# Encoder layer on one core: the filters' second product over 128 rows, and three side products one unit of weights later

## The chip, the cores and the metric

The kernel runs on one core of one Trainium2 chip. The metric is the device time of one execution in microseconds (us). Before the change it is 1980.1 us, the median of three runs (1979.52, 1980.10 and 1980.14 us). The engines are named as the profile names them: PE is the matrix engine's multiplication, PEld its loading of weights, DVE the vector engine, ACT the scalar engine, POOL the GpSimd engine, and SP the engine whose queue issues most transfers.

## What is computed

One layer of an encoder over 256 tokens of 2048 channels, in float32. Cut to its steps:

```
x <- LN1(alpha*x + 0.5*(silu(x@Wg1) * (x@Wu1)) @ Wd1)         # d_ff 5632
h = x;  proj = h @ w_in                                       # 2048 x 6144
v, g1, g2 = split(short_conv(proj[:, :3072]), 3)              # the Hyena group, 1024 channels each
filt = sin-MLP(33 -> 64 -> 64 -> 64)(positions) @ filt_w_out  # 64 x 4096, times a decay
y = v;  for n in 0, 1:  y = g[n] * fftconv(y, filt[n, forward], filt[n, backward], bias[n])
o = differential attention of the other half of proj          # 8 heads
x <- LN2(alpha*x + [rms(y) ; o] @ w_out)
x <- LN3(alpha*x + 0.5*(silu(x@Wg2) * (x@Wu2)) @ Wd2)
```

## The kernel before

All matrices are streamed once from DRAM in 656 **units** of 0.5 MB, in the order of their use. SP's queue fetches a unit (`fetch`, five ahead), and `prepare` splits it three units ahead of its use into a high part (a cast on ACT, L159) and a low part (raw minus high, on DVE, L160). There are four buffers each for the high and the low part, so ACT cannot cast a unit before the unit four places ahead of it has been used up. PE then makes three products of every float32 product: high x high, low x high and high x low.

Work that is not part of the stream is written as Python generators. `tick`, called once for each unit, counts down what a generator last yielded and runs its next piece when the count is 0. So `yield 2` means: let two units pass. A piece's products stand on PE's queue between two units, and PE takes its queue strictly in order. Within that, a scheduler that works by its own estimates sets the exact order on each engine.

Two places matter here.

**The filters** (`filter_gen`) run beside the down projection of the first feed-forward half step. `h` holds the network's 64 outputs for 256 positions twice, in partitions 0 to 63 and again in 64 to 127; `hs` holds its high part in the lower-numbered half and its low part in the other. `fh` and `fl` are the high and low parts of `filt_w_out`, which is loaded into both halves too. For each of eight blocks (four blocks of channels `cc`, two orders `n`) there are two directions `d` and two token halves `j`, and for each of these four a product over all 128 rows (L550), which gives high x high + low x high at once, and then a product over the first 64 rows alone (L551), which gives high x low. All eight of a block stand together on PE's queue. After them DVE multiplies by the decay (L553), and `spectra_mm` takes the filters to the frequency domain (tiles `pr`, `pi`, named `prk`, `pik` here), in twelve products over 128 rows by 256 columns.

**The Hyena group** takes 48 units (`hy<cc>_<s>_<kq>`: four blocks of channels `cc`, in each the sections `s` = 0 for v, 1 for the first gate and 2 for the second, of four units each). `conv_in` (L636 on) makes the short convolution of a section on ACT and DVE (tile `z`, L648), yields, and transposes it on PE into `pt` (L657). For s = 0 it then starts `chain(cc)`: `product("a")` with the first filter, an inverse transform on PE into `py`, a gate, `product("b")` with the second filter, and an inverse transform into `pz` (L725, L726). `product` is: the transform on PE (`pra`, `pia` or `prb`, `pib`), a butterfly on ACT and DVE (`ab`, `cd`), the multiplication by the filter's spectrum, half on POOL (`t2`, `t3`) and half on DVE (`t0`, `t1`), and the real and imaginary results, split into `rh`, `rl`, `ih`, `il` (ACT casts at L97, DVE subtractions at L94). After the last split it yields 3 before the inverse transform. A chain is longer than the 12 units of a block of channels, so product b of one block and product a of the next run side by side, and since `rh`, `rl`, `ih`, `il` have one buffer each, the a product cannot be split before `pz` of the block ahead has been computed.

Of the kernel before, what the change touches and what calls it, by code (L numbers as in the profile page):

```python
# [11 lines left out]
F32 = mybir.dt.float32  # L12
# [16 lines left out]
HID = 64  # L29
EPS = 1e-5  # L30
ALPHA = 2.0 ** 0.25
# [13 lines left out]
def _constants():  # L45
    """Tables that depend on shapes alone. Tokens are cut as l = 2 p + j."""
    f4 = np.float32
    lag = 2 * np.arange(P)[:, None] + np.arange(2)[None, :]
    t = np.linspace(0.0, 1.0, L, dtype=f4)[:, None]
    bands = (EMB - 1) // 2  # L50
    w = f4(2.0 * math.pi) * np.arange(L, dtype=f4)[:, None] / f4(L)
    fr = np.linspace(1e-4, bands - 1, bands, dtype=f4)[None, :]
    z = np.concatenate([t, np.cos(fr * w), -np.sin(fr * w)], axis=-1)
    z_t = np.ascontiguousarray(z[lag.T.reshape(-1)].T, dtype=f4)
    lo, hi = math.log(1e-2) / 1.5, math.log(1e-2) / 0.3
    deltas = np.abs(np.linspace(lo, hi, DH, dtype=f4))
    decay = np.exp(-t * deltas)[lag].astype(f4)
    om = 2.0 * math.pi * (np.arange(P) + 0.5) / NFFT
    ang = lag.T[:, :, None].astype(np.float64) * om[None, None, :]
    fwd = np.stack([np.cos(ang), -np.sin(ang)], axis=1)  # L60
    fwd = np.ascontiguousarray(fwd.transpose(2, 0, 1, 3).reshape(P, 4 * P), dtype=f4)
    inv = np.stack([np.cos(ang), -np.sin(ang)], axis=0) * (2.0 / NFFT)
    inv = np.ascontiguousarray(inv.transpose(3, 0, 1, 2).reshape(P, 4 * P), dtype=f4)
    fi = f4(ROPE_THETA) ** (-np.arange(0, ROT, 2, dtype=f4) / f4(ROT))
    an = (lag.astype(f4)[:, :, None] * fi[None, None, :]).astype(f4)
    cs, sn = np.cos(an), np.sin(an)
    rope = np.stack([np.concatenate([cs, cs], -1), np.concatenate([-sn, sn], -1)], axis=1)
    rope = np.repeat(rope[:, :, :, None, :], 8, axis=3)
    rope = np.ascontiguousarray(rope.reshape(P, 2 * 2 * 8 * ROT), dtype=f4)
    return {"c_zt": z_t, "c_decay": np.ascontiguousarray(decay), "c_fwd": fwd, "c_inv": inv, "c_rope": rope}  # L70
# [3 lines left out]
def kernel(ctx: ExitStack, tc: tile.TileContext, a: dict, out: bass.AP):  # L74
    nc = tc.nc
# [24 lines left out]
    def after(ins, first):  # L100
        """Keeps ins behind first in their engine's queue."""
        tc.add_manual_dep(ins.ins, first.ins.name, mybir.DependencyInfo(mybir.DependencyClass.NoSync, mybir.DependencyReason.DATA), reason="order")
# [3 lines left out]

# [1 line left out]
    units = []  # L108

    def ws_units(tag, w, c0, ws=None):  # L110
        """[4 k-tiles x 256 columns] of one matrix, or of several in turn."""
        for kq in range(KD // 4):
            for m, v in enumerate(ws or [w]):
                units.append((v[0][kq * 512:(kq + 1) * 512, c0:c0 + 256].rearrange("(k p) c -> p k c", p=P), 4, 256, f"{tag}_{kq}_{m}"))

    def as_units(tag, w, c0, kt):
        """[2 k-tiles x 512 columns]."""
        for ku in range(kt // 2):
            units.append((w[0][ku * 256:(ku + 1) * 256, c0:c0 + 512].rearrange("(k p) c -> p k c", p=P), 2, 512, f"{tag}_{ku}"))
# [46 lines left out]

    # work that goes on beside the stream: generators that yield how many units to let pass
    side = []
# [32 lines left out]

# [1 line left out]
    res = const.tile([P, 2, D], F32, name="res")  # L203
# [12 lines left out]

    # per-channel vectors, as columns
    NCONV = 24
# [59 lines left out]
    def warm(n):  # L278
        """Keeps the array's clock up over a wait; the products are not used."""
        ps = bank("ps_warm")  # L280
        for _ in range(n):
            mm(out=ps[:, :P], lhsT=ones, rhs=ones, start=True, stop=True)

    def scale_residual(tag, g, b):
        """res = ALPHA * (res * g + b), or ALPHA * res."""
        for c in range(4):
# [36 lines left out]
    def last_rows(tag, pd, scale):  # L323
        """The last columns of a row block, and its statistics; the first token tile goes ahead."""
        ln = []
        for j in range(2):
            add_rows(pd[j], j, 3, scale)
            ln.append(ln_stats(tag, j))
        if tag == "2":
            warm(WARM)  # L330
        return ln
# [14 lines left out]
    def ws_block(ps, h, lo, kq, between=None):  # L346
        """Left half: hi x hi + lo x hi; right half: hi x lo."""
        for k in range(4):
            kk = kq * 4 + k
            if k == 2 and between is not None:  # L350
                between()
            for t in range(2):
                ts_ = slice(t * P, (t + 1) * P)
                mm(out=ps[t], lhsT=h[:, k, ts_], rhs=xx[:, kk].rearrange("p a l -> p (a l)"), start=kk == 0, stop=False)  # L354
                mm(out=ps[t][:, :L], lhsT=lo[:, k, ts_], rhs=xx[:, kk, 0, :], start=False, stop=kk == KD - 1)  # L355
# [5 lines left out]
    def as_block(pd, lhs, use, n_k):  # L361
        """Rows on the partitions: [tokens, 512 columns]; lhs(k, j) gives the split tokens."""
        for j in range(2):
# [6 lines left out]
    def as_chunk(pd, lhs, n_k, lead=1):  # L370
        """The first token tile is done with the last `lead` units before the second one is."""
        n = n_k // 2
# [4 lines left out]

# [1 line left out]
    def ffn(tag, first, down_side=None, gate_side=None, filler=None, lead=2):  # L379
# [41 lines left out]

# [1 line left out]
    spec = dr.tile([NCC, P, 2, 2, 2 * CH], F32, name="spec")  # L423
# [6 lines left out]
    def spectra_mm(fw_hi, fw_lo, parts_, tag):  # L430
        """[ReE | ReO] and [ImE | ImO] of the transform at half-odd frequencies."""
        pr, pi = bank(f"pr{tag}"), bank(f"pi{tag}")
# [6 lines left out]
    def butterfly(pr, pi, ro, ab, cd):  # L439
        """ab = [Re+ | Re-], cd = [Im+ | Im-]."""  # L440
        nc.scalar.copy(out=ro[:, 0, :], in_=pr[:, CH:])
# [53 lines left out]
    def filter_gen():  # L495
        """Per block of channels and order: the two filters, the even and odd parts about lag 0, their spectra."""
        fw_hi = blk(14).rearrange("p k l -> p (k l)")
# [21 lines left out]
        nc.vector.tensor_copy(out=hs[:HID], in_=hs_hi[:HID].bitcast(F32))  # L519
        sub(nc.vector, hs[HID:], h[HID:], hs_hi[HID:])  # L520
        yield 3
        ft()
# [14 lines left out]
        for i, (cc, n) in enumerate(todo):  # L537
# [7 lines left out]
            for d in range(2):  # L545
                ps = bank(f"pf{i}_{d}")
                for j in range(2):
                    js = slice(j * P, (j + 1) * P)
                    po = ps[:, j * CH:(j + 1) * CH]
                    mm(out=po, lhsT=hs[:, js], rhs=fh[:, d, :], start=True, stop=False)  # L550
                    mm(out=po, lhsT=hs[:HID, js], rhs=fl[:HID, d, :], start=False, stop=True)  # L551
                t = t512(f"fa{i}_{d}")
                nc.vector.tensor_tensor(out=t.rearrange("p j c -> p (j c)"), in0=ps, in1=dec.rearrange("p j c -> p (j c)"), op=ALU.mult)  # L553
                ab.append(t)
            # lag 0 of the backward filter is not used (its sine is 0 too): the skip bias takes its place
            nc.gpsimd.dma_start(out=ab[1][0:1, 0, :], in_=a["hyena_bias"][:, n, cs])
# [20 lines left out]

# [1 line left out]
    def first0(c):  # L579
# [22 lines left out]

# [1 line left out]
    mix = ctx.enter_context(ExitStack())  # L604
# [27 lines left out]
    def conv_in(cc, s, ps):  # L632
        """Short convolution of one block of channels; v and the first gate go to [token, channel]."""
        z = hp.tile([P, 2, 2, P], F32, tag="z2" if s == 2 else "z", name=f"z{cc}_{s}", bufs=2)
# [15 lines left out]
        if s == 2:  # L650
            z2s[cc] = z
            return
        yield 2 if cc == s == 0 else 1
        pt = bank(f"pt{cc}_{s}")
# [13 lines left out]
    def product(tag, u, n):  # L668
        """Spectrum of u times the filter's, as what the even and the odd tokens take of it, split."""
        pr, pi = spectra_mm(fw_hi, fw_lo, (u, u), tag)  # L670
# [24 lines left out]
        split(*i, v[1])  # L695
        yield 3
        prod[tag] = (r, i)
# [3 lines left out]
    def chain(cc, u):  # L701
# [16 lines left out]
        load_spec(cc + 1, 1)  # L718
        # [high | low] parts of the table side by side
        pz = [bank(f"pz{cc}_{t}").rearrange("p (j a l) -> p j a l", j=2, a=2) for t in range(2)]  # L720
# [22 lines left out]
    def rms_rows(sqs, n, tag):  # L743
        """1 / rms per token of the sum of squares over the partitions, in all partitions (PSUM)."""
        ps = bank(f"pss{tag}")
# [60 lines left out]

    # differential attention
    yah = mixp.tile([P, 8, L], F32R, name="yah")
# [130 lines left out]

    # output projection  # L940
    def wo_lhs(k, j):
# [24 lines left out]
    mix.close()  # L966
# [1 line left out]
    ln2 = ln  # L968
# [66 lines left out]
```

## Time and profile before

| | |
|---|---|
| median of three runs | 1980.1 us |
| span of the profiled execution | 1978.4 us |
| PE busy | 1944.3 us (98%) |
| DVE busy | 1217.0 us (62%) |
| ACT busy | 925.6 us (47%) |
| POOL busy | 307.0 us (16%) |
| granted clock, mean | 0.996 of full speed |

The span is from the first to the last instruction; 1.7 us of the median lie around it. Times of rows are counted from the span's start. A row of a timeline gives start, duration, engine, line, operation, tiles and sizes, and in brackets how long the engine was idle before it and what ended that. Products on PE overlap: what one costs in a row of others is the distance from its start to the next start, not the duration that the row gives.

### The profile page before, as it was taken

To read this page: it belongs to the slowest core of one execution; us is meant where nothing else is said; L and a number is where in the kernel's file an instruction comes from. 1 tells how busy PE (TensorE), PEld (TensorE's weight loads), DVE (VectorE), ACT (ScalarE), POOL (GpSimd) and SP (SyncE) were. 2 spreads that over 40 slices of the span, in tenths; PEclk is the share of its full clock that TensorE was granted. 3 is DMA by queue.
4 is the path that set the end of the run, shared out by engine and by line. 5 is a ranking of instruction groups with operands and counts; after the bars stand their busy time and mean duration, and the time that the engine had idled before them with its cause. 6 is when DMAs were issued, how large, how long until landed. Compare 5 with 4: busy or idle time off the path is not lost. (4 is left out here: it accounts for less than half of the span.)

```text
span 1978.4 us, 27114 instructions
## 1 busy us (share of the span) xinstructions
PE 1944.3 (98%) x10292; PEld 1661.0 (84%) x10292; DVE 1217.0 (62%) x1534; ACT 925.6 (47%) x1332; POOL 307.0 (16%) x330
## 2 busy tenths in 40 slices
PE   9999999999999999999999999999999999999996
PEld 7888888888887777888878888888888888888885
DVE  5555556555565655899978666755555555544445
ACT  5444444544444434555555544545444544433332
POOL 5112111121100000212321010311111121100001
PEclk9999999999999999999999999999999999999998
DMA  7666666666666655755575544866666666656663
GB/s 244 189 189 191 192 191 195 190 187 192 194 201 196 202 177 177 237 186 170 173 235 151 160 155 149 279 191 192 188 192 189 190 190 192 190 183 191 189 186 104
DMA packets 293514, 374.33 MB, mean 189 GB/s; under 512 B 13103, under 2 KB 222152, under 8 KB 293384
## 3 DMA queue, kind: packets, MB, share of 16 engines
q1 hardware_dynamic: 288648, 359.80, 59.1%
q0 software_dynamic: 4736, 12.82, 2.1%
q8 instruction: 80, 1.31, 0.3%
q14 instruction: 50, 0.41, 0.1%
HBM read 364.18 MB, written 8.39 MB: 188 GB/s over the span
## 5 line engine op out<-in xcount | busy, mean ns | idle before, releaser
L354 PE MATMUL ps<-xx,hi1g 128*128 128x512 f32 x1408 | 489.5, 391 | 1.3 <-DVE xx L94 0.8
L354 PE MATMUL ps<-xx,hi2g 128*128 128x512 f32 x1408 | 488.6, 391 | 1.1 <-DVE xx L94 1.1
L355 PE MATMUL ps<-xx,lo1g 128*128 128x256 f32 x1408 | 397.4, 282 | 0.3 <-DVE lo1g L160 0.3
L355 PE MATMUL ps<-xx,lo2g 128*128 128x256 f32 x1408 | 397.3, 282 | 0.0
L160 DVE TENSOR_TENSOR lo2g<-raw2g,hi2g 128x1024 fp32r<-128x1024 f32 x176 | 235.1, 1337 | 179.4 <-ACT hi2g L159 179.4
L160 DVE TENSOR_TENSOR lo1g<-raw1g,hi1g 128x1024 fp32r<-128x1024 f32 x176 | 231.5, 1317 | 180.0 <-ACT hi1g L159 179.8
L354 PEld LDWEIGHTS ps<-xx,hi1g 128*128 128x128 f32 x1408 | 264.3, 188 | 57.6 <-DVE xx L94 1.4
L354 PEld LDWEIGHTS ps<-xx,hi2g 128*128 128x128 f32 x1408 | 264.2, 188 | 55.8 <-ACT xt L268 1.3
L159 ACT CAST hi2g<-raw2g 128x1024 fp32r<-128x1024 f32 x176 | 185.2, 1053 | 186.6 <-PE ps L354 176.1
L159 ACT CAST hi1g<-raw1g 128x1024 fp32r<-128x1024 f32 x176 | 185.3, 1053 | 184.8 <-PE ps L354 175.6
L355 PEld LDWEIGHTS ps<-xx,lo1g 128*128 128x128 f32 x1408 | 266.7, 189 | 0.6 <-DVE lo1g L160 0.6
L355 PEld LDWEIGHTS ps<-xx,lo2g 128*128 128x128 f32 x1408 | 266.8, 189 | 0.1
L160 DVE TENSOR_TENSOR lo2d<-raw2d,hi2d 128x1024 fp32r<-128x1024 f32 x88 | 108.5, 1233 | 128.2 <-ACT hi2d L159 128.2
L390 POOL TENSOR_TENSOR hf<-hf,sg 128x256 f32<-128x256 f32 x88 | 65.6, 766 | 765.7 <-DVE hf L359 765.6
L159 ACT CAST hi1d<-raw1d 128x1024 fp32r<-128x1024 f32 x88 | 92.4, 1050 | 155.0 <-PE pd L91 145.1
L159 ACT CAST hi2d<-raw2d 128x1024 fp32r<-128x1024 f32 x88 | 92.6, 1052 | 148.8 <-PE pd L91 145.4
L160 DVE TENSOR_TENSOR lo1d<-raw1d,hi1d 128x1024 fp32r<-128x1024 f32 x88 | 107.7, 1223 | 83.4 <-ACT hi1d L159 83.4
L89 PE MATMUL pd<-hi1d,hh 128*128 128x512 f32 x352 | 140.3, 399 | 0.0
L90 PE MATMUL pd<-lo2d,hh 128*128 128x512 f32 x352 | 139.4, 396 | 0.0
L91 PE MATMUL pd<-hi2d,hl 128*128 128x512 f32 x352 | 139.4, 396 | 0.0
L89 PE MATMUL pd<-hi2d,hh 128*128 128x512 f32 x352 | 139.3, 396 | 0.0
L91 PE MATMUL pd<-hi1d,hl 128*128 128x512 f32 x352 | 139.3, 396 | 0.0
(371 smaller groups left out, 3073.2 us busy)
## 6 DMA issues: line engine op xcount, KB each, us to landing
raw1g<-in_ffn_w_gate_dram SPq DMA_DIRECT2D x88, 512.0 KB, 3.5
raw1g<-in_ffn_w_up_dram SPq DMA_DIRECT2D x88, 512.0 KB, 3.6
raw1d<-in_ffn_w_down_dram SPq DMA_DIRECT2D x88, 512.0 KB, 3.7
raw2g<-in_ffn_w_gate_dram SPq DMA_DIRECT2D x88, 512.0 KB, 3.5
raw2g<-in_ffn_w_up_dram SPq DMA_DIRECT2D x88, 512.0 KB, 3.5
raw2d<-in_ffn_w_down_dram SPq DMA_DIRECT2D x88, 512.0 KB, 3.9
rawhy<-in_w_in_dram SPq DMA_DIRECT2D x48, 512.0 KB, 3.6
rawat<-in_w_in_dram SPq DMA_DIRECT2D x48, 512.0 KB, 3.9
```

The costliest lines, as they stand in the source:

```text
L89: mm(out=o, lhsT=lh, rhs=rh, start=start, stop=False)
L90: mm(out=o, lhsT=lh, rhs=rl, start=False, stop=False)
L91: mm(out=o, lhsT=ll, rhs=rh, start=False, stop=stop)
L159: i1 = nc.scalar.copy(out=hi, in_=raw)
L160: i2 = nc.vector.tensor_tensor(out=lo, in0=raw, in1=hi.bitcast(F32), op=ALU.subtract)
L354: mm(out=ps[t], lhsT=h[:, k, ts_], rhs=xx[:, kk].rearrange("p a l -> p (a l)"), start=kk == 0, stop=False)
L355: mm(out=ps[t][:, :L], lhsT=lo[:, k, ts_], rhs=xx[:, kk, 0, :], start=False, stop=kk == KD - 1)
L390: nc.gpsimd.tensor_tensor(out=hf, in0=hf, in1=sg, op=ALU.mult)
```

## The change

The diff also empties comments and docstrings, and four lines added behind L520 give later lines numbers that are higher by four. What is left:

```diff
@@ filter_gen
         nc.vector.tensor_copy(out=hs[:HID], in_=hs_hi[:HID].bitcast(F32))
         sub(nc.vector, hs[HID:], h[HID:], hs_hi[HID:])
+
+        hz = xx[:, 1, 0, :]
+        nc.vector.memset(hz[HID:].bitcast(F32), 0.0)
+        nc.vector.tensor_copy(out=hz[:HID], in_=hs_hi[:HID].bitcast(F32))
         yield 3
...
                     mm(out=po, lhsT=hs[:, js], rhs=fh[:, d, :], start=True, stop=False)
-                    mm(out=po, lhsT=hs[:HID, js], rhs=fl[:HID, d, :], start=False, stop=True)
+                    mm(out=po, lhsT=hz[:, js], rhs=fl[:, d, :], start=False, stop=True)
@@ conv_in
-        yield 2 if cc == s == 0 else 1
+        yield 3 if cc == s == 0 else 2
         pt = bank(f"pt{cc}_{s}")
@@ product
         split(*i, v[1])
-        yield 3
+        yield 4
         prod[tag] = (r, i)
```

The second product now runs over all 128 rows, of which the lower 64 hold zeros in `hz`. The transposes `pt` stand one unit later on PE's queue, and the inverse transforms `py` and `pz` one unit later after their product. What follows them moves along: `chain` starts one unit later, and its end three units later.

Three places on the queues show it. The first is on PE, at the first transposes of the Hyena group. Before:

```order
L354 MATMUL ph0_1_1_6923<-xx_70,hihy0_1_3_0_6961 128x512
L355 MATMUL ph0_1_1_6923<-xx_70,lohy0_1_3_0_6962 128x256
L657 MATMUL pt0_0_7045<-ident_83,z0_0_6934 128x128 x4
L354 MATMUL ph0_2_0_7035<-xx_70,hihy0_2_0_0_6991 128x512
L355 MATMUL ph0_2_0_7035<-xx_70,lohy0_2_0_0_6992 128x256
```

and with the change:

```order
L354 MATMUL ph0_2_1_7038<-xx_70,hihy0_2_0_0_6993 128x512
L355 MATMUL ph0_2_1_7038<-xx_70,lohy0_2_0_0_6994 128x256
L661 MATMUL pt0_0_7078<-ident_83,z0_0_6936 128x128 x4
L354 MATMUL ph0_2_0_7037<-xx_70,hihy0_2_1_0_7015 128x512
L355 MATMUL ph0_2_0_7037<-xx_70,lohy0_2_1_0_7016 128x256
```

The transposes stood behind unit `hy0_1_3` and stand behind the next one, `hy0_2_0`.

The second is on DVE, where product b of the first block of channels (`abb0`, `cdb0`) meets product a of the second (`aba1`, `cda1`). Before:

```order
L443 TENSOR_TENSOR abb0_7556<-prb0_7519,rob0_7555 128x256
L444 TENSOR_TENSOR abb0_7556<-prb0_7519,rob0_7555 128x256
L445 TENSOR_TENSOR cdb0_7557<-rob0_7555,pib0_7520 128x256
L446 TENSOR_TENSOR cdb0_7557<-rob0_7555,pib0_7520 128x256
L681 TENSOR_TENSOR t0b0_7607<-abb0_7556,res_69 128x512
L682 TENSOR_TENSOR t1b0_7608<-cdb0_7557,res_69 128x512
L691 TENSOR_TENSOR t2b0_7609<-t2b0_7609,t3b0_7610 128x512
L160 TENSOR_TENSOR lohy2_0_2_0_7604<-rawhy2_0_2_0_7483,hihy2_0_2_0_7603 128x1024
L443 TENSOR_TENSOR aba1_7618<-pra1_7569,roa1_7617 128x256
L444 TENSOR_TENSOR aba1_7618<-pra1_7569,roa1_7617 128x256
```

and with the change:

```order
L443 TENSOR_TENSOR abb0_7632<-prb0_7567,rob0_7631 128x256
L444 TENSOR_TENSOR abb0_7632<-prb0_7567,rob0_7631 128x256
L445 TENSOR_TENSOR cdb0_7633<-rob0_7631,pib0_7568 128x256
L446 TENSOR_TENSOR cdb0_7633<-rob0_7631,pib0_7568 128x256
L359 TENSOR_TENSOR pc19_7651<-ph1_2_1_7424,pc19_7651 128x256
L685 TENSOR_TENSOR t0b0_7681<-abb0_7632,res_69 128x512
L686 TENSOR_TENSOR t1b0_7682<-cdb0_7633,res_69 128x512
L443 TENSOR_TENSOR aba1_7643<-pra1_7586,roa1_7642 128x256
L444 TENSOR_TENSOR aba1_7643<-pra1_7586,roa1_7642 128x256
```

A unit of weights was prepared between the two (`lohy2_0_2`, L160); now they follow each other directly. On PE's queue `prb0` stood behind unit `hy1_2_1` and `pra1` behind `hy1_2_2`; now both stand behind `hy1_2_3`. For the pairs b1 with a2 and b2 with a3 the distance was two units and is now one.

The third is on PE, where `pz` of the first block of channels ends and `py` of the second follows. Before, the end of `pz0`:

```order
L725 MATMUL pz0_1_7806<-iv_6739,ihb0_7707 128x256
L726 MATMUL pz0_1_7806<-iv_6739,ilb0_7708 128x256
L354 MATMUL ph2_1_0_7765<-xx_70,hihy2_1_1_0_7738 128x512
L355 MATMUL ph2_1_0_7765<-xx_70,lohy2_1_1_0_7739 128x256
L354 MATMUL ph2_1_1_7766<-xx_70,hihy2_1_1_0_7738 128x512
L355 MATMUL ph2_1_1_7766<-xx_70,lohy2_1_1_0_7739 128x256
```

and with the change:

```order
L729 MATMUL pz0_1_7884<-iv_6741,ihb0_7764 128x256
L730 MATMUL pz0_1_7884<-iv_6741,ilb0_7765 128x256
L89 MATMUL py1_7902<-rha1_7733,iv_6741 128x256
L661 MATMUL pt2_0_7915<-ident_83,z2_0_7775 128x128 x4
L354 MATMUL ph2_2_0_7874<-xx_70,hihy2_2_0_0_7832 128x512
L355 MATMUL ph2_2_0_7874<-xx_70,lohy2_2_0_0_7833 128x256
L354 MATMUL ph2_2_1_7875<-xx_70,hihy2_2_0_0_7832 128x512
L355 MATMUL ph2_2_1_7875<-xx_70,lohy2_2_0_0_7833 128x256
L354 MATMUL ph2_2_0_7874<-xx_70,hihy2_2_0_0_7832 128x512
L355 MATMUL ph2_2_0_7874<-xx_70,lohy2_2_0_0_7833 128x256
L90 MATMUL py1_7902<-rla1_7734,iv_6741 128x256
```

Before, all sixteen products of unit `hy2_1_1` stood between the end of `pz0` and the first product of `py1`; now the first product of `py1` follows `pz0` at once, and the second one comes after four transposes and six products of a unit.

## Rows read from the trace of the kernel before

**Rows 1.** Busy time of the engines by stretch: down projection, Hyena group
```profile
core 0: us, PE busy (x) PEld busy (x) DVE busy (x) ACT busy (x) POOL busy (x), PEclk, DMA share, GB/s
497.00:700.00 203.00, 203.00 (x897) 161.35 (x896) 122.11 (x152) 84.77 (x106) 14.52 (x24) 1.00 0.64 196
812.00:960.00 148.00, 142.42 (x862) 126.81 (x861) 142.37 (x262) 80.02 (x129) 29.41 (x21) 1.00 0.58 179
```

**Rows 2.** Waits of PE: line waited for, us in total, times, longest
```profile
PE pt L657 <- DVE z L648: 4.5, 2, 2.6
...
PE py L90 <- DVE rla L94: 1.1, 1, 1.1
...
PE pw L900 <- DVE e L896: 1.0, 1, 1.0
```

**Rows 3.** Timeline of PE at the first of eight filter blocks
```profile
515.68 0.40 PE L91 MATMUL pd<-hi1d,hl 128*128 128x512 f32 x1
515.91 0.28 PE L550 MATMUL pf<-xx 128*128 128x256 f32 x1
516.12 0.38 PE L551 MATMUL pf<-xx 64*128 64x256 f32 x1
516.43 0.38 PE L550 MATMUL pf<-xx 128*128 128x256 f32 x1
...
518.00 0.38 PE L551 MATMUL pf<-xx 64*128 64x256 f32 x1
518.31 0.50 PE L89 MATMUL pd<-hi1d,hh 128*128 128x512 f32 x1
518.65 0.39 PE L90 MATMUL pd<-lo1d,hh 128*128 128x512 f32 x1
```

**Rows 4.** Tile `pf`: duration in ns (least, median, most), first and last start
```profile
L551 PE MATMUL pf<-xx x32: 380/382/383, 516.1 to 695.2; 64*128 64x256 f32 x32
```

**Rows 5.** Timeline of PE at the twelve products of a spectrum
```profile
532.41 0.28 PE L89 MATMUL prk<-xx 128*128 128x256 f32 x1
...
533.72 0.28 PE L91 MATMUL pik<-xx 128*128 128x256 f32 x1
533.84 0.40 PE L89 MATMUL pd<-hi1d,hh 128*128 128x512 f32 x1
```

**Rows 6.** Timeline of PE's weight loads, in the same spectrum
```profile
532.53 0.19 PEld L91 LDWEIGHTS prk<-xx 128*128 128x128 f32 x1
532.64 0.19 PEld L89 LDWEIGHTS prk<-xx 128*128 128x128 f32 x1
```

**Rows 7.** Timeline of PE at attention scores, products over 64 rows
```profile
1024.20 0.28 PE L90 MATMUL psc<-ql,qh 64*128 64x256 f32 x1
1024.32 0.28 PE L91 MATMUL psc<-qh,ql 64*128 64x256 f32 x1
1024.53 0.50 PE L89 MATMUL pa0v<-hiat,xx 128*128 128x512 f32 x1
```

**Rows 8.** Timeline of DVE where `hs` is made
```profile
488.23 0.28 DVE L519 CAST xx<-xx 64x256 fp32r<-64x256 f32 x1
```

**Rows 9.** Timeline of ACT ahead of the first convolution
```profile
810.50 0.62 ACT L97 CAST fw_hi<-c_fwd_raw 128x512 fp32r<-128x512 f32 x1 [4.81 <-DMA c_fwd_raw<-in_c_fwd_dram]
```

**Rows 10.** Timeline of DVE, then of PE: a low part made, and first used
```profile
876.23 1.22 DVE L160 TENSOR_TENSOR lohy<-rawhy,hihy 128x1024 fp32r<-128x1024 f32 x1
...
878.95 0.28 PE L355 MATMUL ph<-xx,lohy 128*128 128x256 f32 x1
```

**Rows 11.** Timeline of ACT at `py1`
```profile
885.72 0.62 ACT L97 CAST rha<-v0a 128x512 fp32r<-128x512 f32 x1
```

**Rows 12.** Timeline of DVE in the first burst
```profile
863.71 1.78 DVE L682 TENSOR_TENSOR t1b<-cdb,res 128x512 f32<-128x512 f32 x1
865.42 0.68 DVE L691 TENSOR_TENSOR t2b<-t2b,t3b 128x512 f32<-128x512 f32 x1
```

**Rows 13.** Timeline of POOL in the first burst
```profile
863.19 1.75 POOL L680 TENSOR_TENSOR t3b<-cdb,res 128x512 f32<-128x512 f32 x1
```

## Prediction, made before the changed kernel was run

> **What bounds the kernel now.** I first read busy time by stretch [rows 1]. In the down projection, where the filters are made, PE is busy for all of its 203.00 us, at the full granted clock (1.00, the 2.4 GHz level): there any time taken from PE's queue comes off the end, as long as DVE (122.11 us) and the transfers (a share of 0.64) keep up, and both have room. In the Hyena group PE is busy for 142.42 of 148 us, so it loses 5.6 us there, and DVE is busy for 142.37 us: the second engine is nearly full. Then I read PE's waits [rows 2]: two of the transposes `pt` wait for the convolution (4.5 us together, the longest 2.6), `py` once for the low part of its operand (1.1 us), the weights of attention `pw` once (1.0 us). Behind the first layer norm these are the only waits of 1 us and more up to the output projection, and the change touches the first two. Last I read single rows of PE where the filters stand [rows 3], since a busy PE need not be a PE at its pace.
>
> **The second product over 128 rows.** A block's eight products run from 515.91 to 518.31 us: 2.40 us, 0.30 each. The products ahead of them come every 0.23 us (515.68 to 515.91) though they have twice the columns. The product behind them costs 518.65 - 518.31 = 0.34 us instead of 0.23 [rows 3]. What makes them slow? The twelve products of a spectrum have the same 256 columns, all over 128 rows: 532.41 to 533.84 us, 1.43 us, 0.119 each [rows 5]. Nor are 64 rows slow by themselves: the attention scores have 64 rows too, and two in a row are 0.12 us apart (1024.20 to 1024.32), but the last one, ahead of a product over 128 rows, takes 0.21 (1024.32 to 1024.53) [rows 7]. So the price lies in changing from 128 rows to 64 and back, about 0.1 us or more each time, and a block changes eight times. With 128 rows throughout I price the eight as the spectrum's: 8 x 0.119 = 0.95 us, and the product behind them at 0.23. Saved: (2.40 - 0.95) + (0.34 - 0.23) = 1.56 us a block. The 32 products over 64 rows are alike to 3 ns (380 to 383) [rows 4], four to a block, so eight blocks save 8 x 1.56 = **12.5 us**, all on the path. The bounds are 0 (rival 3 below) and these 12.5, which leave no change of shape in a block; I take 12.5, since the spectrum's row is of the same shape in the same stage.
>
> The change adds a memset and a cast of 64 x 256 to DVE, once. The nearest row is the cast of that size, 0.28 us [rows 8]; two make 0.6 us, ahead of the next unit's low part. DVE is idle for 80 us of the 203 us that follow, and low parts are made three units ahead, so I cost it at nothing; without that cover it would be 0.6 us. The memset waits until the gate products have read block 1 of `xx`, as the instructions ahead of it already wait for block 0, so nothing new is queued behind it.
>
> Here a rule of the Trainium skill speaks against the change; the rows of the same stage come first. In the spectrum a load of weights takes 0.19 us and the next one starts 0.11 us after it began, while products run without a break [rows 5, 6]: loads over 128 rows do lie beside products over 128 rows. The Trainium skill, page "TensorE: Matmul & The Clock Gate", section "Part 3: Packing small matmuls — row/col tiling", says that a load of weights overlaps a product in flight only when the two use different row groups. By that rule the trace of the spectrum could not look as it does.
>
> **The side products one unit later.** A unit is sixteen products in pairs of 0.23 + 0.12 us, 2.8 us. The two waits of `pt` (2.6 and 1.9) are each shorter than that, and DVE's order ahead of these convolutions is the same. The first comes from ACT, which stood for 4.81 us waiting for a table's transfer [rows 9] with the convolution queued behind it; that transfer is issued at the same unit as before. So both waits go: **-4.5 us**, with 0.2 left over at most.
>
> Against it stands what moves together. Product b0 used to start one unit ahead of product a1; now both start behind the same unit (second place of the change). Their work on DVE comes as one burst, in the stretch where DVE is full. Before, that burst cut the lead of the low parts to 878.95 - (876.23 + 1.22) = 1.5 us [rows 10]. Now b0 comes two units later against the stream and a1 one, and the units' due times stay. If the burst ends one unit (2.8 us) later, the lead becomes 1.5 - 2.8 = -1.3: PE waits **1.3 us** for a low part (bounds 0 and 3). Then `py1` follows `pz0` with no unit between (third place). Its operand `rha1` has one buffer, read by `pz0` to its end, so ACT casts it only then: 0.62 us [rows 11] and the way there and back, **0.8 us**. The next product of `py1` needs `rla1`, behind which DVE may be on time (0) or three low parts late (3 x 1.13 = 3.4, each row of 1.22 overlapping the next by 0.09); I take the middle, **1.7 us**. Sum 3.8 us, against 1.1 us for the wait shown plus about 0.5 in smaller gaps of the same `py1` now: a net loss of **2.2 us** (from -1.6 to +3.9 or so). The order of DVE's queue was made by the scheduler for this, which is why the second product of `py1` stands behind six of a unit: that hides part of it.
>
> The pairs b1/a2 and b2/a3 come one unit apart, as b0/a1 was, but their `pz` and `py` stand a unit later than that one's did, which is more than the 1.6 us that it lost: 0, with 1.6 each as the upper bound. The chain's end, three units later, falls further into the attention heads; the 1.0 us of `pw` may go or double: 0 (from -1 to +1). Transfers move with their generators (the spectra of the next block of channels and the reload of `res` on SP's queue); the spectra keep over four units until they are read, so they cost nothing. No stretch here is idle long enough to have lost the clock before: it stood at 1.00 over the 148 us with the 2.6 us wait in them [rows 1].
>
> Sum: -12.5 - 4.5 + 2.2 = -14.8. The profiled span is 1978.4 us, 1.7 less than the median of the runs; I take the difference off the median: 1980.1 - 14.8 = **1965.3 us**.
>
> **The rivals.** (1) *The bursts cost nothing.* If DVE keeps up, `py1` loses its 1.6 us as well and `pw` its 1.0: -12.5 - 7.1, 1960.5 us. For it: leads of low parts are far longer outside the bursts. Against it: DVE's 142.37 of 148 us. (2) *The bursts cost more.* All upper bounds: -12.5 - 4.3 + 3.9 + 3.2 + 1.0 = -8.7, 1971.4 us. For it: while POOL multiplies, DVE's multiplications slow down, 1.78 us against 0.68 for the same size once POOL is through [rows 12, 13], and POOL's work for two products now comes in one go. (3) *The filters gain nothing.* If a load over 128 rows has to wait for the product before it, each of the eight costs 0.19 + 0.12 = 0.31 us, a block 2.48, and only the side products' 2.3 us are left: 1977.8 us. That is the time by the rule of the Trainium skill named above; [rows 5, 6] speak against it. (4) *Slower.* DVE becomes the bound of the Hyena group: POOL's two products hold the memory path for 6.1 us in each of the three bursts, and six operations of DVE there take 1.1 us more each (1.78 against 0.68, rows 12), 6.6 us a burst, and every `py` waits as `py1` did, 1.6. That decides once the low parts' lead is used up at a burst's start. 3 x 8.2 = 24.6, less 12.5 and 4.5: +7.6, 1987.7 us. Against it: the lead was never below 1.5 us, and only the first pair falls together entirely.
>
> **How the numbers follow.** A measurement of this kernel can tell about 0.2% (4 us) from no change. The forecast, 1962.5 to 1968.5 us: 58%. Rival 1, below that: 14%. Rival 2, 1968.5 to 1975: 21%. Rival 3: 4%. Rival 4: 3%. The range from 1961 to 1971.5 us leaves out some half of rival 1, a quarter of rival 2, and rivals 3 and 4: 19%. Faster by over 0.2% are the forecast and rivals 1 and 2: 0.93; same is rival 3: 0.04; slower is rival 4: 0.03.
>
> **What would show it.** In the timeline of PE at the filters all eight products should show 128 rows and lie 0.12 us apart, a block 0.95 us, the product behind it 0.23. A block of 2.4 us would prove rival 3 and cost 12.5 us. In the waits, `pt <- z` should be gone; `py` should wait for `rha` and `rla`, once each, some 0.8 and 1.7 us, at `py1` alone; waits of L355 for a low part ahead of `pz0` should be near 1.3 us. If `py` waits in all of the last three blocks, the sum of the bursts was too small; if none is left, rival 1 holds. A granted clock below 1.00 in the Hyena group would mean a wait long enough to cost PE its clock, which I have not priced.

## The result and the profile after

The median is **1966.53 us** (1966.24 to 1968.11, four runs) against 1979.91 us (1979.52 to 1980.14, four runs) of the kernel before on the same chip: the ratio is 0.993, with a 95% interval from 0.9918 to 0.9941. The kernel is faster by 13.4 us; 14.8 were forecast, and the time lies inside the range. The profiled execution has a span of 1964.9 us, 13.5 less than before.

In the kernel after, the two products of a block are L554 and L555, `pt` is L661, `pz` L729 and L730, `pw` L904.

First PE at the first filter block (start, duration, engine, line, operation, tiles, sizes):

```profile
515.74 0.39 PE L91 MATMUL pd<-hi1d,hl 128*128 128x512 f32 x1
515.97 0.28 PE L554 MATMUL pf<-xx 128*128 128x256 f32 x1
516.09 0.28 PE L555 MATMUL pf<-xx 128*128 128x256 f32 x1
...
516.80 0.28 PE L555 MATMUL pf<-xx 128*128 128x256 f32 x1
516.92 0.40 PE L89 MATMUL pd<-hi1d,hh 128*128 128x512 f32 x1
517.16 0.39 PE L90 MATMUL pd<-lo1d,hh 128*128 128x512 f32 x1
```

Against [rows 3], all eight products show 128 rows. They take 516.92 - 515.97 = 0.95 us instead of 2.40, and the product behind them 517.16 - 516.92 = 0.24 us instead of 0.34. So a block saves 1.55 us, and eight of them 12.4.

The loads of weights of the same eight products (engine PEld):

```profile
515.97 0.19 PEld L555 LDWEIGHTS pf<-xx 128*128 128x128 f32 x1
516.09 0.19 PEld L554 LDWEIGHTS pf<-xx 128*128 128x128 f32 x1
516.21 0.19 PEld L555 LDWEIGHTS pf<-xx 128*128 128x128 f32 x1
```

A load of 0.19 us starts every 0.12 us, each together with a product that uses the weights loaded before, over the same 128 rows. The rule on which rival 3 stood (the Trainium skill, page "TensorE: Matmul & The Clock Gate", section "Part 3: Packing small matmuls — row/col tiling": a load overlaps a product in flight only when their row groups differ) does not hold here; by it the block would have cost some 2.5 us.

The loads of the kernel before, at the same place, look different:

```profile
516.12 0.18 PEld L551 LDWEIGHTS pf<-xx 64*128 64x128 f32 x1 [0.25 <-issue]
516.43 0.19 PEld L550 LDWEIGHTS pf<-xx 128*128 128x128 f32 x1
```

There each load starts only with the product that uses it (516.12 and 516.43, as the products of [rows 3]), and not with the product ahead of it. So where the number of rows changes, the load lies open: 0.18 to 0.19 us each time, and with the 0.12 us of the product 0.31. That is the sum that rival 3 made for the kernel after; it was the kernel before that paid it.

Then the waits of PE in the kernel after (line waited for, us in total, times, longest):

```profile
PE py L89 <- ACT rha L97: 1.9, 1, 1.9
...
PE pw L904 <- DVE e L900: 1.6, 1, 1.6
PE py L90 <- DVE rla L94: 1.5, 1, 1.5
...
PE ph L355 <- DVE lohy L160: 0.5, 1, 0.5
```

Against [rows 2], the 4.5 us of `pt` are gone. New are the first line (at `py1`) and the last (a low part ahead of `pz0`). The wait of `py` for `rla` has grown from 1.1 to 1.5 us and stands at another place, `py2`. `pw` went from 1.0 to 1.6.

Last the busy times by stretch (PE, PEld, DVE, ACT, POOL, granted clock, DMA share, GB/s). The Hyena group begins 12 us earlier than before, so the 148 us are taken from 800 on:

```profile
497.00:700.00 203.00, 203.00 (x950) 167.43 (x949) 128.21 (x159) 89.67 (x111) 14.57 (x24) 1.00 0.67 208
800.00:948.00 148.00, 144.02 (x868) 127.94 (x867) 141.81 (x262) 80.85 (x129) 27.07 (x21) 1.00 0.58 177
```

In the down projection PE stays the bound while more work passes in the same 203 us: x950 instructions instead of x897 [rows 1]. In the Hyena group PE is busy for 144.02 us instead of 142.42; DVE is still the second full engine (141.81).

**How the rest of the difference is found.** The idle time that a wait shows is less than what PE loses there. In a row of others a product over 256 columns is followed after 0.119 us by the next start, one over 512 columns after 0.233, and a transpose by the next one after 0.109. What a start lies behind that is called *lost* below. Here are PE's rows at the two places where `py` waits now; first `py1`:

```profile
877.20 0.28 PE L730 MATMUL pz<-iv,ilb 128*128 128x256 f32 x1
879.39 0.39 PE L89 MATMUL py<-rha,iv 128*128 128x256 f32 x1 [1.91 <-ACT rha L97]
879.62 0.60 PE L661 MATMUL pt<-ident,z 128*128 128x128 f32 x4
...
880.98 0.28 PE L355 MATMUL ph<-xx,lohy 128*128 128x256 f32 x1
881.33 0.39 PE L90 MATMUL py<-rla,iv 128*128 128x256 f32 x1
```

Lost: 879.39 - 877.20 - 0.12 = 2.07 us for `rha`, and 881.33 - 880.98 - 0.12 = 0.23 us for `rla`. Ahead of `pz0`, a product of a unit loses 872.75 - 871.86 - 0.233 = 0.66 us to its low part, here on PE and then on DVE:

```profile
871.86 0.39 PE L354 MATMUL ph<-xx,hihy 128*128 128x512 f32 x1
872.75 0.38 PE L355 MATMUL ph<-xx,lohy 128*128 128x256 f32 x1 [0.50 <-DVE lohy L160]
...
871.49 1.21 DVE L160 TENSOR_TENSOR lohy<-rawhy,hihy 128x1024 fp32r<-128x1024 f32 x1
```

The sum at this pair is 2.96 us. Why `rha` came so late is seen on ACT in the same stretch:

```profile
878.18 0.37 ACT L358 COPY pc<-ph 128x256 f32<-128x256 f32 x1 [0.65 <-DVE z L652]
878.45 0.38 ACT L734 COPY zs<-pz 128x256 f32<-128x256 f32 x1
878.71 0.63 ACT L97 CAST rha<-v0a 128x512 fp32r<-128x512 f32 x1
```

The cast of `rha` was not next on ACT's queue when `pz0` had ended: two copies stood ahead of it, and the first of them waited 0.65 us for DVE's convolution. Then `py2`, on PE and on DVE:

```profile
920.25 0.28 PE L89 MATMUL py<-rha,iv 128*128 128x256 f32 x1
922.02 0.39 PE L90 MATMUL py<-rla,iv 128*128 128x256 f32 x1 [1.50 <-DVE rla L94]
```

```profile
919.03 2.34 DVE L160 TENSOR_TENSOR lohy<-rawhy,hihy 128x1024 fp32r<-128x1024 f32 x2
921.30 0.68 DVE L94 TENSOR_TENSOR rla<-v0a,rha 128x512 fp32r<-128x512 f32 x1
```

PE loses 1.65 us, since DVE made two low parts of units, 2.34 us, ahead of `rla`. With 0.14 us at `ila`, a few products further on, the pair costs 1.8 us.

### The profile page after: what moved, and what is told of

Same layout as the page of the kernel before. It is cut to its first block, busy times and chain, and to the rows that moved or that the text cites. A ratio compares the mean times of both kernels' runs of the same rounds, so it can differ in the third digit from the quotient of the medians.

```text
span 1964.9 us, 27112 instructions
## 1 busy us (share of the span) xinstructions
PE 1932.7 (98%) x10292; PEld 1656.2 (84%) x10292; DVE 1215.2 (62%) x1536; ACT 925.8 (47%) x1332; POOL 306.0 (16%) x330
## 5 line engine op out<-in xcount | busy, mean ns | idle before, releaser
L160 DVE TENSOR_TENSOR lo2g<-raw2g,hi2g 128x1024 fp32r<-128x1024 f32 x176 | 235.1, 1337 | 179.3 <-ACT hi2g L159 177.7
L160 DVE TENSOR_TENSOR lo1g<-raw1g,hi1g 128x1024 fp32r<-128x1024 f32 x176 | 232.2, 1320 | 178.8 <-ACT hi1g L159 178.8
L160 DVE TENSOR_TENSOR lo2d<-raw2d,hi2d 128x1024 fp32r<-128x1024 f32 x88 | 108.3, 1231 | 128.3 <-ACT hi2d L159 128.3
L160 DVE TENSOR_TENSOR lo1d<-raw1d,hi1d 128x1024 fp32r<-128x1024 f32 x88 | 107.2, 1222 | 71.0 <-ACT hi1d L159 71.0
```

What stands on the lines that cost most here:

```text
L160: i2 = nc.vector.tensor_tensor(out=lo, in0=raw, in1=hi.bitcast(F32), op=ALU.subtract)
```

## The experiments

Three questions were put: what each half of the change does by itself, what makes the filter products slow, and what makes the side products wait.

### Each half alone

e1 keeps the filters' change and leaves both yields as they were before. Against the kernel before:

```diff
+        hz = xx[:, 1, 0, :]
+        nc.vector.memset(hz[HID:].bitcast(F32), 0.0)
+        nc.vector.tensor_copy(out=hz[:HID], in_=hs_hi[:HID].bitcast(F32))
...
-                    mm(out=po, lhsT=hs[:HID, js], rhs=fl[:HID, d, :], start=False, stop=True)
+                    mm(out=po, lhsT=hz[:, js], rhs=fl[:, d, :], start=False, stop=True)
```

> The kernel before with the second filter product over 128 rows, and the three yields as they were. Theory (the price lies in changing from 128 rows to 64 and back): eight blocks of 1.56 us each go from PE's path and nothing else moves, so 12.4 us less than before, about 1967.5 us; the two waits of pt (4.5 us), the one of py1 (1.1) and that of pw (1.0) stay. Rival (part of those 12.4 us was slack that the faster down projection hands to a later wait): 1969 to 1972 us, with a new wait of PE for a unit of weights behind the filters.

Measured: 1969.28 us (1967.67 to 1970.61, five runs) against 1981.73 of the kernel before (1979.64 to 1984.03, 15 runs of this chip, with which e1 to e4 are compared); ratio 0.9937 (0.9925 to 0.995). The medians are 12.45 us apart, what the filter blocks give. The expected 1967.5 us had been reckoned from the 1979.9 us of the runs beside the result. The span of the profiled execution is 1967.1 us, 11.3 less than before. `pt` waits twice and `py` once, as in the kernel before:

```profile
PE pt L661 <- DVE z L652: 3.7, 2, 1.9
...
PE py L90 <- DVE rla L94: 1.1, 1, 1.1
```

So no new wait behind the filters takes anything back. In this execution part of the 12.4 us is given back elsewhere: the first filter block starts 0.7 us later (516.59 us), and behind the first wait of `pt` PE ran some 3 us at the lower level of its clock (last section).

e2 makes only the other half, both yields, in the kernel before:

```diff
-            yield 2 if cc == s == 0 else 1
+            yield 3 if cc == s == 0 else 2
...
-        yield 3
+        yield 4
```

> The kernel before with the three yields raised and the filter products as they were. Theory (the waits of pt go, 4.7 us by starts of products, but the bursts give 3.5 us back: py1 +1.3, py2 +1.8, pw +0.6, py3 -0.3): 1.0 to 1.3 us less than before, about 1978.8 us. Rival (the yields bring their full 4.5 to 5 us, and the filters bring less than 12.4): about 1975.2 us.

Measured: 1980.43 us (1979.07 to 1981.64, 11 runs); ratio 0.9995 (0.9986 to 1.0004). No change can be told, and the 1.0 to 1.3 us that were expected of the side products' move can't be ruled out either. Its waits repeat those of the kernel after, to the tenth:

```profile
PE py L89 <- ACT rha L97: 1.9, 1, 1.9
...
PE py L90 <- DVE rla L94: 1.5, 1, 1.5
```

In its profiled execution the side products lose 4.74 us from the Hyena group to the end of the last `py`, the kernel before 6.80 and the kernel after 4.93, so 2.1 us are gained there, and 0.6 of them go to `pw`. That the span was 1978.5 us nevertheless comes from 775 to 800 us, where PE's granted clock was 0.93 and in the kernel before 1.00, ahead of anything that the yields move.

### One yield at a time, beside the filters

e3 keeps `hz` and the yields of `conv_in`, and takes the product's back to 3. e4 keeps `hz` and the product's yield of 4, and takes those of `conv_in` back. Against the kernel after:

```diff
 # e3
-        yield 4
+        yield 3
 # e4
-            yield 3 if cc == s == 0 else 2
+            yield 2 if cc == s == 0 else 1
```

> The changed kernel with the yield of product back at 3; the transposes stay one unit later. Theory (what the product's yield does is to push the pairs b0/a1, b1/a2 onto each other or next to py, and it costs): no wait of py2, py1 about 1.6 us as before the change, no wait of pt, so about 2 us less than the changed kernel, 1964.3 us. Rival (the bursts come from the transposes' yield, since it starts the chains later): the waits of py1 and py2 stay at 3 and 1.8 us, time as the changed kernel's 1966.5 or above, since pz and py come a unit earlier.

> The changed kernel with the yields of conv_in back at 2 and 1; the inverse transforms stay one unit later. Theory: the waits of pt are back (2.6 and some of the 1.9 us), and the burst of b0 with a1 stays, so 12.4 us less than before and then 0 to 3 us more: 1968 to 1971 us. Rival (the bursts come from the transposes' yield): py1 and py2 wait for nothing, 1966 us or less.

Measured, e3: **1963.10 us** (1963.02 to 1963.31, four runs), ratio 0.9906 (0.9893 to 0.992); span 1961.2 us, 3.7 less than the kernel after. e4: 1971.75 us (1969.28 to 1972.18, five runs), ratio 0.9947 (0.9935 to 0.996); span 1967.5 us. Against e1, on the same chip, the yields of `conv_in` gain 6.2 us and the product's yield costs 2.5. So the yields of `conv_in` are the whole gain, and the product's yield is a loss. (e4 lies 0.75 us above the range expected; its profiled execution was the fastest of the five, at a mean granted clock of 0.996 where the other four had 0.995.) The waits of e3:

```profile
PE py L90 <- DVE rla L94: 1.0, 2, 0.9
```

and of e4:

```profile
PE pt L661 <- DVE z L652: 2.4, 1, 2.4
...
PE py L90 <- DVE rla L94: 1.8, 3, 0.8
PE py L89 <- ACT rha L97: 1.7, 1, 1.7
```

Without the product's yield `py` no longer waits for `rha` at all, and `pt` does not wait either. With that yield alone, `py` waits in all of the last three blocks and `pt` still once.

### What makes the filter products slow

e5 is the kernel before with the same products over 128 and 64 rows, in another order: two over 128 rows, then two over 64, and this twice. A block then changes its number of rows four times instead of eight. The lines added:

```diff
+            pss = [bank(f"pf{i}_{d}") for d in range(2)]
+            for j in range(2):
+                js = slice(j * P, (j + 1) * P)
+                for d in range(2):
+                    mm(out=pss[d][:, j * CH:(j + 1) * CH], lhsT=hs[:, js], rhs=fh[:, d, :], start=True, stop=False)
+                for d in range(2):
+                    mm(out=pss[d][:, j * CH:(j + 1) * CH], lhsT=hs[:HID, js], rhs=fl[:HID, d, :], start=False, stop=True)
```

> The kernel before with the eight products of a block in another order: per token half two products over 128 rows (one per direction), then two over 64 rows. The shape changes four times a block instead of eight; all products stay as they are, and the yields too. Theory (a change of shape costs): half of the 1.56 us a block goes, 0.75 us, 6 us in all, about 1974 us; two products of equal shape in a row lie 0.12 us apart. Rival (each product over 64 rows is slow by itself, in this stage): all eight stay 0.3 us apart or the 64-row ones do, 1978 to 1980 us.

Measured: 1974.83 us (1972.29 to 1975.84, six runs) against 1979.94 (1978.87 to 1982.77, ten runs); ratio 0.9967 (0.9955 to 0.9979). PE at the first block (x2 is two products in one row):

```profile
516.16 0.40 PE L549 MATMUL pf<-xx 128*128 128x256 f32 x2
516.49 0.50 PE L551 MATMUL pf<-xx 64*128 64x256 f32 x2
516.92 0.50 PE L549 MATMUL pf<-xx 128*128 128x256 f32 x2
517.35 0.50 PE L551 MATMUL pf<-xx 64*128 64x256 f32 x2
517.78 0.50 PE L89 MATMUL pd<-hi1d,hh 128*128 128x512 f32 x1
518.11 0.40 PE L90 MATMUL pd<-lo1d,hh 128*128 128x512 f32 x1
```

The same eight products take 1.62 us, and the one behind them 0.33. Above the 0.95 + 0.23 us of a block without a change that is 0.77 us for four changes, 0.19 each. In the kernel before it was 2.40 + 0.34 - 1.18 = 1.56 us for eight changes [rows 3], 0.195 each. So the price sits in the change, not in the 64 rows, and it is the same for both orders. (One thing expected was missed: the two products of a pair lie 0.22 us apart and not 0.12, 516.49 and 516.71, since the first of them starts together with its open load. Into the changed product it is 0.21, and the two distances together are 0.19 above 2 x 0.12.) Eight blocks save 8 x (2.40 + 0.34 - 1.62 - 0.33) = 6.3 us; the span is shorter by 4.5, since behind a wait of `pt` the clock fell in this execution too (the columns of the busy times by stretch):

```profile
810.90:812.80 1.90, 1.90 (x7) 1.62 (x6) 1.90 (x3) 0.59 (x2) 0.00 (x0) 0.50 0.57 200
```

### What makes the side products wait

e6 gives `rh` and `rl` two buffers, so that `rha` need not wait until `pz` has been computed. Against the kernel after:

```diff
-        r = ht(f"rh{tag}", "rh", F32R), ht(f"rl{tag}", "rl", F32R)
+        r = ht(f"rh{tag}", "rh", F32R, 2), ht(f"rl{tag}", "rl", F32R, 2)
```

> The changed kernel with two buffers each for rh and rl instead of one, so that the a product's real part can be split before pz of the block ahead has been computed. Theory (at py1 PE waits 1.9 us for the cast of rha because that cast may only start when pz0 has read the one buffer): the wait of py1 for rha goes, and those for rla shrink at py1 and py2; 2 to 3.5 us less than the changed kernel, 1963 to 1964.5 us. Rival (ACT and DVE are simply behind in the burst, whatever the buffers): py1 waits for ih, il or z instead, and the time stays within 0.7 us of the changed kernel's 1966.5.

Measured: 1968.42 us (1966.72 to 1969.36, five runs), ratio 0.9937 (0.9925 to 0.995); span 1966.7 us, 1.8 more than the kernel after. Neither the theory (2 to 3.5 us less) nor the rival (within 0.7) has the time right. Counted from start to start, the waits of this stage cost 4.9 us, as in the kernel after; most of the 1.8 is the clock, which fell behind the longest of them (last section). The wait for `rha` is gone, as it had to be, and another stands in its place, a little earlier:

```profile
PE ph L355 <- DVE lohy L160: 2.5, 1, 2.5
```

DVE's rows ahead of it show why (start, duration):

```profile
871.01 0.68 DVE L94 TENSOR_TENSOR rla<-v0a,rha 128x512 fp32r<-128x512 f32 x1
871.61 0.68 DVE L94 TENSOR_TENSOR ilb<-v1b,ihb 128x512 fp32r<-128x512 f32 x1
...
873.67 1.21 DVE L160 TENSOR_TENSOR lohy<-rawhy,hihy 128x1024 fp32r<-128x1024 f32 x1
```

`rla` could now be made ten microseconds before `py1` asked for it, and it was, ahead of the low part for which PE stood until 874.94 us. In the kernel after that low part started at 871.49 us and came 0.66 us late. The theory that the single buffer of `rh` and `rl` sets the loss fell: the time is lacking on DVE, and this buffer only changes who waits for it.

e7 moves the starts apart instead. In the kernel after, the number of units between a product b and product a of the next block was 0, 1 and 1; it is made 2 everywhere:

```diff
-            yield 3 if cc == s == 0 else 2
+            yield 3 if s == 0 else 2
...
-        yield 4
+        yield 3
```

> Filters over 128 rows; the transposes of v two units later than before for the second to fourth block of channels and one for the first, so that every chain starts at the same place in its block; the yield of product back at 3. Every product b and the next product a are then two units apart, every pz and the next py too. Theory: no wait of pt and none of py1 or py2: 12.4 + 4.7 + 1.7 + 0.3 = 19 us less than before, 1961 us, with pw at 1.0 to 1.6 us. Rival (DVE is full in this stage and hands the waits on, to low parts of weights or to later transposes): 1963 to 1966 us.

Measured: **1961.87 us** (1961.70 to 1962.14, four runs), ratio 0.9907 (0.9893 to 0.992); span 1960.3 us. Of the waits, those of `pt`, of `py` and of the low parts are gone; one of a gate's transform has come:

```profile
PE prb L90 <- DVE u2l L94: 1.0, 1, 1.0
...
PE pw L904 <- DVE e L900: 0.4, 1, 0.4
```

Counted from start to start PE loses 1.36 us at that transform: two of DVE's operations ahead of it took 2.00 and 2.17 us instead of 1.21 and 1.12, while POOL worked beside them. So some of the loss is handed on, as the rival said, but most is gone: e7 is 18.1 us faster than the kernel before, and its slowest run is 4.1 us under the fastest of the kernel after (the two were not timed side by side; of the profiled executions, the spans are 1960.3 and 1964.9). From e3 it cannot be told: each against the kernel before on its own chip, e3 gains 18.6 us (0.9906) and e7 18.1 (0.9907).

Put side by side, five kernels show what goes with the loss of `py`. The distance is counted in units between the start of `pz` and that of `py` of the next block; lost is PE's time at `py` and at low parts around it:

| kernel | `pz0`, `py1`: distance, lost | `pz1`, `py2`: distance, lost |
|---|---|---|
| before | 1 unit, 1.66 us | 2 units, 0 |
| after | 0 units, 2.96 us | 1 unit, 1.80 us |
| e4 (product's yield alone) | 0 units, 2.46 us | 1 unit, 1.41 us |
| e3 (yields of `conv_in` alone) | 1 unit, 1.18 us | 2 units, 0 |
| e7 (starts two units apart) | 2 units, 0 | 2 units, 0 |

At these two pairs, in all five, two units cost nothing, one unit 1.2 to 1.8 us, none 2.5 to 3.0. At the third pair, where the last units of the Hyena group have run out and those of attention follow, this order does not hold: two units apart it loses 0.27 us before, 0.48 in e3 and 0 in e7, one unit apart 0 after and 1.10 in e4. What sets the loss there stays open.

## Why the prediction was right, and where it was not

**The filters: right to 0.1 us.** Forecast 12.5, measured 8 x 1.55 = 12.4 us, all on the path. The step that carried it was to leave the durations aside and to take the distance from start to start, from products of the same shape in the same stage. The reason given (the change of the number of rows, "about 0.1 us or more each time") was the right one but low: it is 0.19 us each time, by e5 and by the kernel before, as long as the load of weights that lies open there. The forecast did not need that number, since it removed all eight. The memset and the cast cost nothing that shows: PE is busy for all of the 203.00 us.

**`pt`: right.** Forecast -4.5 with at most 0.2 left. The two waits had cost PE 4.88 us from start to start, and 0.17 are left: -4.7.

**The pair b0/a1: the sum too large, its parts exchanged.** Forecast a loss of 3.8 us less the old 1.6. Measured 2.96 less the old 1.66, so +1.3 instead of +2.2. The low part cost 0.66 us instead of 1.3: the lead fell from 1.5 us [rows 10] to -0.6 (the product was due at 871.86 + 0.23 = 872.09 us, the low part ended at 872.70), not to -1.3. `rha` cost 2.07 instead of 0.8: the step "ACT casts it only then" took the cast to be next on ACT's queue, and two copies stood ahead of it, one of them waiting for DVE. `rla` cost 0.23 instead of 1.7: while PE waited for `rha`, DVE caught up. Three terms that were added share one shortage, so what one of them took, the next did not pay again. The bound of +3.9 was also added up wrongly: the bounds as stated (3, 0.8 and 3.4, less 1.6) give +5.6, and rival 2 would have been 1.7 us slower. The measured +1.3 lies under both.

**The pairs b1/a2 and b2/a3: wrong for the first of them.** "0, with 1.6 each as the upper bound" was forecast; b1/a2 lost 1.80 us, b2/a3 nothing (and the 0.27 us that it lost before are gone). The step that failed is the argument that `pz` and `py` standing a unit later gave more than b0/a1 had lost. Being late by a unit bought nothing; at these pairs the loss goes with the distance between the two, as the table shows: one unit cost 1.66 us at b0/a1 before and 1.80 at b1/a2 now.

**`pw`: mis-sized.** 0 was forecast (from -1 to +1), the wait grew by 0.6 us. It was also 1.6 in e2 and e6, 1.2 in e3 and 0.4 in e4 and e7. What sets it was not followed up.

**The sum.** -12.4 - 4.7 + 1.3 + 1.8 - 0.3 + 0.6 = -13.7, against 13.5 less in the span. The side products brought 1.3 us instead of 2.3, mainly by `py2`. That is a step of rival 2 (bursts cost more), in one place instead of three. That the sum came so near is in part luck: 0.9 us too much at the first pair hid half of the 1.8 too little at the second. Rival 2's reason, that POOL slows DVE more when two products come in one go, is not what differs. By an estimate from DVE's rows between the first `pt` and the last `py`, what operations took above the shortest of their kind (where that is over 0.15 us) adds up to 12.2 us before, 11.7 after, 10.2 in e3, 12.1 in e4 and 12.5 in e7. The clock, which the prediction had named as the thing not priced, stood at 1.00 through the Hyena group in this execution. That a wait of 2.6 us had not lost it before was the reading of one execution: in e5 the same wait of `pt` was followed by 0.50.

That the time is lacking on DVE, and that the single buffer of `rh` and `rl` does not set the loss, is shown by e6; that it goes when the work of two products is moved apart is shown by e7; that the product's yield makes it is shown by e3, e4 and the table. Not shown is which of two things in a pair matters more, that the two products' butterflies fall together or that `pz` and `py` do: the yields move both at once, and no kernel here moved one alone.

## What to carry to other kernels

Where products over different numbers of rows alternate on the tensor engine, compare their starts with a row of equal ones elsewhere in the trace; padding the smaller with zeros to the same number of rows can be cheaper than doing half the work, and putting equal ones side by side gets half of it. Before moving several side jobs by a step each, count how far each pair of them comes apart in the new order: a move that ends one wait can be undone by two jobs that now ask the same nearly full engine in the same unit. A wait for a buffer that a second buffer would end says little about the time, if the engine behind it is full; look at what that engine would do instead.

## What was not expected of the hardware

**A single wait can cost PE its clock for some microseconds, in some executions.** In e1, e5 and e6, the product behind one of 512 columns started 0.43 us after it instead of 0.233, for some 3 us behind one wait. The rows by stretch, of e1 (ahead of the `pt` wait's end, and behind it):

```profile
800.00:803.00 3.00, 1.20 (x9) 0.92 (x7) 3.00 (x7) 2.92 (x5) 0.00 (x0) 1.00 0.35 116
804.00:807.00 3.00, 3.00 (x11) 2.57 (x10) 3.00 (x6) 1.35 (x3) 0.00 (x0) 0.50 0.61 198
```

and of e6 (the wait for the low part, and behind it):

```profile
872.00:875.00 3.00, 0.45 (x4) 0.13 (x2) 3.00 (x8) 1.71 (x2) 0.00 (x0) 0.99 0.01 4
875.00:878.00 3.00, 3.00 (x10) 2.61 (x11) 3.00 (x8) 0.60 (x1) 0.00 (x0) 0.50 0.54 172
```

0.50 is the 1.2 GHz level. PE had been idle for 1.8 us before it in e1, where the clock fell about 1 us after the wait's end, and for 2.55 us in e6, where it fell as the wait ended. Each such stretch of 3 us does the work of 1.5. The kernel before shows that this need not follow:

```profile
813.00:816.00 3.00, 0.38 (x3) 0.18 (x3) 3.00 (x8) 2.82 (x5) 0.00 (x0) 1.00 0.28 91
816.00:819.00 3.00, 3.00 (x19) 2.67 (x19) 3.00 (x4) 0.99 (x3) 0.00 (x0) 1.00 0.62 188
```

It was idle for longer than e1, and the clock stayed at 1.00. Nor does it need so long a wait: in e2 the clock fell at 785.8 us, behind waits of 0.53 and 1.10 us, and the kernel before, with waits as long at the same place, kept it. The spread between runs fits a loss that only some executions have: kernels with a wait of 1.8 us or more in this group spread over 1.9 us (after, four runs) to 4.4 us (before, 15 runs; the four beside the result lay within 0.6), and e3 and e7, which have none above 1.3 us, over 0.3 and 0.4 us. So taking out such a wait is worth its length and this risk. The mean granted clock that is on record for every run agrees in part: of e6, the two runs at 0.997 took 1966.72 and 1966.94 us, the three at 0.995 and 0.996 took 1968.42 to 1969.36; of e5, the fastest had 0.996 and the two slowest 0.995. It does not say where the clock fell; only the profiled executions show that.

**The change of the number of rows has one price in two orders**: 0.195 us over eight changes a block, 0.19 over four, some 1.6 times the 0.119 us of a product over 256 columns. It agrees with the time of one load of weights (0.18 to 0.19 us), which starts together with the product ahead of it when both are over the same number of rows, and only with its own product when the number changes.
